# First additions of the norms' sums on VectorE, and the memory input loaded in four pieces

## The chip, the core and the metric

The kernel runs on one core of a Trainium2 chip. The core has five engines that run their own instruction lists side by side: TensorE for matmuls (PE in the rows, with its weight loads as PEld), VectorE (DVE), ScalarE (ACT), GpSimd (POOL) and SyncE (SP), which here only starts transfers. The engines wait for each other on semaphores, and each takes its instructions in order, so one that waits holds up all behind it. The metric is the time of one execution on the device in microseconds (us), as a median over runs.

## What is computed

Three blocks in float32, with 256 tokens of width 1024. Cut to what the change touches (the bodies of the attentions and of the state space model are left out):

```
def first_block(x, mem, ...):
    h = rmsnorm(x, mix_norm_g)
    y_s5 = s5(h @ w_in[u]); y_m = mlstm(h @ w_in[q, k, v, o, i, f])
    merged = sigmoid(gate) * (y_s5 @ w_br_s5) + sigmoid(gate) * (y_m @ w_br_m)
    x = x + merged @ w_out
    h = rmsnorm(x, x_norm_g)
    x = x + cross_attn(h, rmsnorm(mem, mem_norm_g), x_wq, x_wkv, x_wo)
    x = x + conv_ffn(rmsnorm(x, f_norm_g), ...)
    return rmsnorm(x, final_norm_g)
def even_block(x):  # differential and dilated attention, layer norm, conv FFN, layer norm
def odd_block(x):   # sparse and latent attention, layer norm, conv FFN, layer norm
```

`rmsnorm` divides by the root of the mean square over the 1024 features; `layer_norm` also takes the mean away.

## The kernel before

Activations lie feature-major: 8 tiles of 128 features by 256 tokens, so that x is `[128, 8, 256]`. A matmul in float32 is done as three matmuls in a rounded format: each operand is split in a high and a low part, and high x high, high x low and low x high are added up. For weights `wload` (L313) does it: SyncE fetches 128 x 1024 of a weight (512 KB) into `raw`, ScalarE copies it to `hi` (L321), VectorE makes `lo = raw - hi` (L322). `raw` has four buffers, `hi` and `lo` three each, so a weight is copied when the matmuls of the third before it are done. TensorE uses the parts at L329 to L331 (L338 to L340 for the token-major form), 24 matmuls for each pair.

A norm's sums over the 1024 features cross the partitions, and TensorE does that by a matmul with a column of ones (L469, tile `m`). Ahead of it `squares` has ScalarE square the tiles (L502, L506), two at a time for three pairs and two single ones, and `folded` (L484) adds them up: the first two pairs on GpSimd (L488), the third on VectorE (L490), the two halves (L492), a single one (L494). It is called 13 times: five root mean square norms, and four layer norms with two sums each. After L469 the reciprocal root is formed, and TensorE broadcasts it as a row over the partitions (L513), which becomes `rs` or `lnrow`.

The first block's mixer has, in this order on TensorE, the q and k groups (their results in `msg`, evicted by VectorE at L1706 and convolved into `mcv`), the groups that give v and the input and forget gates (`w_vif`, evicted to `vm` and `ifs`), and the rest of v and the output gate (`w_tm`, the first weight being hi_1026). Between them stand the small matmuls of the S5 state (L796 to L822), fed by VectorE (`so`, `hs`, L771, L772) and copied out by ScalarE (`CR`, `CN`, `KS`, `gs`, `gm`).

At its end `w_out` is applied in four column groups. Beside them `cross` (L981) begins: one transfer brings `mem`, 1 MB, on SyncE (L983). `rms_defer` (L581) then makes the split operand of the memory: `oh = mem * gain` on ScalarE (L583) and `ol` on VectorE (L584) for each of 8 tiles, and the squares, whose sums TensorE takes at L469 after the fourth column group. The projections use `oh`, `ol` right away, and the row is multiplied in afterwards. `mem` is a tile of a pool whose memory the mixer had, so its transfer waits until the mixer's last reader is done.

Who does what, and on which engine, is written in the program; the order of each engine's instructions is not. A planner (`schedule_with_timeline_sim=True`, L1861) walks the whole program with its own costs for every instruction and transfer and puts each engine's list in the order in which its model has them ready, with a higher priority for the weights (`WPRI`) and the layer norms (`LPRI`). A change in one line can so move instructions in other places.

Of the kernel before, what the change touches and what calls it, by code (L numbers as in the profile page):

```python
# [257 lines left out]
def _program(ctx, tc, nc, a, offs, dump):  # L258
    V, ACT, G, PE = nc.vector, nc.scalar, nc.gpsimd, nc.tensor
# [16 lines left out]
    def T(pl, shape, tag, dt=F32, **k):  # L276
        cnt[0] += 1
        return pl.tile(list(shape), dt, tag=tag, name="%s_%d" % (tag, cnt[0]), **k)

    mult, add, sub = ALU.mult, ALU.add, ALU.subtract  # L280
    stt = V.scalar_tensor_tensor
    tt = V.tensor_tensor
# [159 lines left out]
    def gemm_tm(name, ch, xh, xl, evac, cw=256):  # L442
        for j, c in enumerate(ch):
            if cw == 256:
                ps = T(pg, [P, 2, 256], "g")
                pt = [ps[:, t, :] for t in range(2)]
            else:
                pt = [T(pg, [P, cw], "g") for t in range(2)]
            step = 4 if cw == 256 else 3
            for k0 in range(0, 8, step):  # L450
                k1 = min(8, k0 + step)
                w = wload(name, c, cw * k0, cw * k1)
                for t in range(2):
                    tm_mm(pt[t], w, range(k0, k1), cw, t, xh, xl,
                          start=k0 == 0 and (t == 0 or cw > 256), stop=k1 == 8, skip=cw == 256)
            evac(j, ps if cw == 256 else pt)
# [27 lines left out]
    def folded(pairs, singles):  # L484
        if not pairs:
            return list(singles)
        acc = T(tp, [P, 2, S], "sqa", bufs=2)
        G.tensor_tensor(acc, pairs[0], pairs[1], op=add)  # L488
        for p in pairs[2:]:
            tt(acc, acc, p, op=add)  # L490
        one = acc[:, 0, :]
        tt(one, one, acc[:, 1, :], op=add)  # L492
        for p in singles[:-1]:
            tt(one, one, p, op=add)  # L494
        return [one, singles[-1]]
# [27 lines left out]
    def rms_cols(x, kt, eps, at=None):  # L523
        st = T(*(at or (pm,)), [P, 2], "g" if at else "m")
        col_sums(st, [folded(*squares(x, kt))])
        return rstd_cols(st, 2, kt * P, eps, "rms")

    def split(src, h, l, scale=None):
        if scale is None:
            ACT.copy(h, src)  # L530
            tt(l, src, h, op=sub)  # L531
        else:
            act(h, src, AF.Copy, scale=scale)
            stt(l, src, scale, h, op0=mult, op1=sub)
# [46 lines left out]
    def rms_defer(x, kt, g, eps, h, l, at=None):  # L581
        for k in range(kt):
            act(h[:, k, :], x[:, k, :], AF.Copy, scale=g[:, k:k + 1])  # L583
            stt(l[:, k, :], x[:, k, :], g[:, k:k + 1], h[:, k, :], op0=mult, op1=sub)  # L584
        r = rms_cols(x, kt, eps, at)
        rb = row_bcast([r[:, 0:1], r[:, 1:2]], at)
        rs = T(tp, [P, S], "rs")
        ACT.copy(rs, rb)
        return rs, r
# [13 lines left out]
    def bc2(rs):  # L603
        return bc(rs[:, None, :], [P, 2, S])

    def act_split():
        return T(hp, [P, 8, S], "xh", F32R), T(hp, [P, 8, S], "xl", F32R)
# [36 lines left out]
    def residual(x, xn):  # L644
        def ev(j, ps):
            tt(xn[:, 2 * j:2 * j + 2, :], ps, x[:, 2 * j:2 * j + 2, :], op=add)

        def single(n, ps):
            with tc.high_priority(LPRI):
                tt(xn[:, n, :], ps, x[:, n, :], op=add)  # L650

        def joint(n, ps):
            tt(xn[:, n, :], ps[:, 0, :], x[:, n, :], op=add)
            tt(xn[:, n, :], ps[:, 1, :], xn[:, n, :], op=add)
        return dict(evac=ev, single=single, joint=joint)
# [319 lines left out]
    def transpose_out(src_blocks, pl=None, tag="a"):  # L975
        tr = T(pl or pa, [P, 4, P], tag)
        for k, b in enumerate(src_blocks):
            PE.transpose(tr[:, k, :], b, ident)
        return tr

    def cross(ap_, x1):  # L981
        mem = T(ap_, [P, 8, S], "mem")
        nc.sync.dma_start(mem, a["mem"])  # L983
        memh, meml = T(ap_, [P, 8, S], "oh", F32R), T(ap_, [P, 8, S], "ol", F32R)
        ms_, mc_ = rms_defer(mem, 8, C["mem_norm_g"], 1e-6, memh, meml)
        kh, kl = [T(ap_, [P, 8, S], "k" + s, F32R) for s in "hl"]
        vh, vl = [T(ap_, [P, 2, D], "v" + s, F32R) for s in "hl"]

        def scaled(ps, rs, h, l):
            t = T(tp, [P, 2, S], "sq", bufs=3)  # L990
            tt(t, ps, bc2(rs), op=mult)
            split(t, h, l)

        def ev_k(j, ps):
            s2 = slice(2 * j, 2 * j + 2)
            scaled(ps, ms_, kh[:, s2, :], kl[:, s2, :])

        def ev_v(j, ps):
            for t in range(2):
                c = slice(j * 256, (j + 1) * 256)  # L1000
                split(ps[:, t, :], vh[:, t, c], vl[:, t, c], mc_[:, t:t + 1])

        gemm_pairs("x_wk", range(4), 8, memh, meml, ev_k)
        gemm_tm("x_wv", range(4), memh, meml, ev_v)
        xh, xl = act_split()
        rs, _ = rms_defer(x1, 8, C["x_norm_g"], 1e-6, xh, xl)
        qh, ql = [T(ap_, [P, 8, S], "q" + s, F32R) for s in "hl"]
        oh, ol = T(ap_, [P, 8, S], "oh", F32R), T(ap_, [P, 8, S], "ol", F32R)

        def x_scores(h, ps):  # L1010
            s2 = slice(2 * h, 2 * h + 2)
            scaled(ps, rs, qh[:, s2, :], ql[:, s2, :])
            sp = T(pa, [P, 2, S], "a")
            for t in range(2):
                for k in range(2 * h, 2 * h + 2):
                    tok = slice(t * P, (t + 1) * P)
                    mm(sp[:, t, :], qh[:, k, tok], kh[:, k, :], start=k % 2 == 0, stop=False)
                    mm(sp[:, t, :], qh[:, k, tok], kl[:, k, :], start=False, stop=False)
                    mm(sp[:, t, :], ql[:, k, tok], kh[:, k, :], start=False, stop=k % 2 == 1)
            nm = T(sm, [P, 2], "xnm")  # L1020
            V.reduce_max(nm, sp, axis=AX.X, negate=True)
            ts(nm, nm, 1.0 / 16, None, op0=mult)
            p = T(ap_, [P, 2, S], "xp", bufs=2)
            den = T(sm, [P, 2], "xden")
            for t in range(2):
                act(p[:, t, :], sp[:, t, :], AF.Exp, bias=nm[:, t:t + 1], scale=1.0 / 16, accum_out=den[:, t:t + 1])
            V.reciprocal(den, den)
            for t in range(2):
                ts(p[:, t, :], p[:, t, :], den[:, t:t + 1], None, op0=mult)
            return p  # L1030

        def x_out(h, p):
            tr = transpose_out([p[:, t, m * P:(m + 1) * P] for m in range(2) for t in range(2)])
            pT = T(ap_, [P, 2, 2, S], "xpT", F32R, bufs=2)
            split(tr.rearrange("p (m t) b -> p m (t b)", m=2), pT[:, 0], pT[:, 1])
            o = T(pm, [P, 2, S], "m")
            for d in range(2):
                for m in range(2):
                    c = slice(h * 256 + d * P, h * 256 + (d + 1) * P)
                    mm(o[:, d, :], vh[:, m, c], pT[:, 0, m, :], start=m == 0, stop=False)  # L1040
                    mm(o[:, d, :], vh[:, m, c], pT[:, 1, m, :], start=False, stop=False)
                    mm(o[:, d, :], vl[:, m, c], pT[:, 0, m, :], start=False, stop=m == 1)
            split(o, oh[:, 2 * h:2 * h + 2, :], ol[:, 2 * h:2 * h + 2, :])

        held = []

        def ev(h, ps):
            held.append((h, x_scores(h, ps)))
            if h >= 1:
                x_out(*held.pop(0))  # L1050

        gemm_pairs("x_wq", range(4), 8, xh, xl, ev)
        x_out(*held.pop(0))
        x2 = T(xp, [P, 8, S], "x")
        gemm_pairs("x_wo", range(4), 8, oh, ol, **residual(x1, x2))
        return x2

    def ln_stats(z):
        with tc.high_priority(LPRI):
            st = T(pm, [P, 4], "m")  # L1060
            col_sums(st, [folded(*tiles(z, 8)), folded(*squares(z, 8))])
        return st
# [726 lines left out]
    with ExitStack() as ph:  # L1789
        x2 = cross(pool(ph, "cx", 1), x1)  # L1790
# [75 lines left out]
```

## Time and profile before

| | us |
|---|---|
| runs shown, median of 3 | 1204.42 (1202.92 to 1205.2) |
| profiled execution | 1202.35 |
| its span, first to last instruction | 1200.6 |
| mean granted TensorE clock (1 is full) | 0.992 |

| engine | busy us | share | instructions |
|---|---|---|---|
| TensorE | 1160.7 | 97% | 8794 |
| VectorE | 911.7 | 76% | 1757 |
| ScalarE | 712.8 | 59% | 1301 |
| GpSimd | 73.4 | 6% | 80 |

The busy share is an average over stages. Where a stage has TensorE busy throughout, no other engine can be what bounds it; where TensorE has a hole, the row gives the instruction that it waited for. Times in the rows count from the start of the span.

### The profile page before, as it was taken

The numbers are of one execution on the slowest core, as the hardware profiler recorded it, in microseconds if no ns is written. First come the engines' busy times: TensorE is split into PE (matmuls) and PEld (weight loads), VectorE is DVE, ScalarE is ACT, GpSimd is POOL, SyncE is SP. The second block draws the span as 40 slices with busy tenths as digits, with TensorE's granted clock in tenths as the row PEclk, the third lists the DMA queues.
The fourth block names the chain that finished last, engine by engine and source line by source line (L and its number), as shares of the span: only waits on it lengthen the run. The fifth ranks groups of instructions, "written<-read, shape, count | busy, mean of one in ns | idle before, by whom it ended". The sixth has DMA issues, their size and how long they took to land.

```text
span 1200.6 us, 22550 instructions
## 1 busy us (share of the span) xinstructions
PE 1160.7 (97%) x8794; PEld 1076.0 (90%) x8794; DVE 911.7 (76%) x1757; ACT 712.8 (59%) x1301; POOL 73.4 (6%) x80
## 2 busy tenths in 40 slices
PE   7999999999999999999999899999999999999997
PEld 6889989999999999899988888888988789888886
DVE  8979856866689887666564898876697768988754
ACT  5684644655566765446355686654685666776541
POOL 4400000100000000000001000001000001000010
PEclk9999999999999999999999999999999999999999
DMA  7524535654356555656522546666863125665561
GB/s 260 166 71 143 166 116 179 221 181 157 103 177 195 182 181 175 191 167 232 170 92 93 191 161 193 187 175 197 284 215 118 57 70 190 191 203 188 168 199 35
DMA packets 61273, 199.35 MB, mean 166 GB/s; under 512 B 8502, under 2 KB 12398, under 8 KB 60910
## 3 DMA queue, kind: packets, MB, share of 16 engines
q1 hardware_dynamic: 54864, 191.60, 49.8%
q10 hardware_dynamic: 6302, 6.32, 1.7%
q8 instruction: 69, 1.13, 0.4%
q14 instruction: 38, 0.31, 0.1%
HBM read 196.28 MB, written 1.60 MB: 165 GB/s over the span
## 4 chain that ended last, share of the span: by engine, by line
PE 87%; DVE 6%; ACT 4%; issue 2%; DMA 1%; POOL 0%; SPq 0%; DVEq 0%; ACTq 0%
PE a L408 11%; PE g L330 10%; PE g L329 10%; PE g L331 10%; PE g L408 8%; PE a L410 6%; PE g L410 4%; PE a L329 3%; PE a L330 3%; PE a L331 3%; PE g L340 2%; PE g L338 2%; PE g L339 2%; DVE lo L322 2%; PE m L1167 1%
## 5 line engine op out<-in xcount | busy, mean ns | idle before, releaser
L321 ACT CAST hi<-raw 128x1024 fp32r<-128x1024 f32 (+3 forms) x359 | 363.9, 1020 | 312.9 <-PE g L330 102.1
L322 DVE TENSOR_TENSOR lo<-raw,hi 128x1024 fp32r<-128x1024 f32 (+3 forms) x359 | 427.5, 1196 | 153.4 <-ACT hi L321 147.8
L329 PE MATMUL g<-xh,hi 128*128 128x256 f32 (+1 forms) x616 | 177.0, 288 | 8.7 <-ACT xh L583 8.4
L330 PE MATMUL g<-xl,hi 128*128 128x256 f32 (+1 forms) x624 | 179.5, 288 | 0.2
L331 PE MATMUL g<-xh,lo 128*128 128x256 f32 (+1 forms) x616 | 175.8, 286 | 1.2 <-DVE lo L322 1.2
L329 PEld LDWEIGHTS g<-xh,hi 128*128 128x128 f32 x616 | 118.2, 192 | 10.2 <-ACT xh L583 8.7
L330 PEld LDWEIGHTS g<-xl,hi 128*128 128x128 f32 x624 | 120.1, 192 | 1.4 <-DVE xl L584 0.7
L408 PE MATMUL a<-nhl,hi 128*128 128x512 f32 x336 | 119.0, 398 | 1.2 <-DVE sq L1110 1.2
L331 PEld LDWEIGHTS g<-xh,lo 128*128 128x128 f32 x616 | 117.7, 191 | 2.0 <-DVE lo L322 1.6
L410 PE MATMUL a<-nhl,lo 128*128 128x256 f32 x336 | 93.9, 279 | 0.0
L408 PE MATMUL a<-mx,hi 128*128 128x512 f32 x264 | 92.5, 396 | 0.0
L408 PE MATMUL g<-nhl,hi 128*128 128x512 f32 x240 | 83.8, 394 | 0.0
L408 PEld LDWEIGHTS a<-nhl,hi 128*128 128x128 f32 x336 | 63.6, 189 | 15.9 <-issue 1.4
L410 PE MATMUL a<-mx,lo 128*128 128x256 f32 x264 | 73.2, 279 | 0.0
L408 PE MATMUL g<-mx,hi 128*128 128x512 f32 x198 | 69.7, 397 | 0.0
L410 PE MATMUL g<-nhl,lo 128*128 128x256 f32 x240 | 66.5, 278 | 0.7 <-DVE lo L322 0.7
L410 PEld LDWEIGHTS a<-nhl,lo 128*128 128x128 f32 x336 | 63.7, 190 | 0.1
L408 PEld LDWEIGHTS a<-mx,hi 128*128 128x128 f32 x264 | 49.3, 188 | 11.5
L410 PE MATMUL g<-mx,lo 128*128 128x256 f32 x198 | 55.4, 280 | 0.0
L408 PEld LDWEIGHTS g<-nhl,hi 128*128 128x128 f32 x240 | 44.9, 188 | 10.2
L329 PE MATMUL a<-nhl,hi 128*128 128x256 f32 x176 | 50.2, 285 | 3.4 <-ACT sqa L1092 2.8
L330 PE MATMUL a<-nhl,hi 128*128 128x256 f32 x176 | 50.0, 284 | 1.0 <-DVE nhl L531 1.0
(637 smaller groups left out, 3088.3 us busy)
## 6 DMA issues: line engine op xcount, KB each, us to landing
raw<-g_up SPq DMA_DIRECT2D x88, 512.0 KB, 3.8
raw<-f_up SPq DMA_DIRECT2D x44, 512.0 KB, 3.4
raw<-g_dn SPq DMA_DIRECT2D x32, 512.0 KB, 3.6
raw<-w_fm SPq DMA_DIRECT2D x27, 512.0 KB, 3.6
raw<-ev_fm SPq DMA_DIRECT2D x20, 512.0 KB, 4.0
raw<-f_dn SPq DMA_DIRECT2D x16, 512.0 KB, 3.7
raw<-od_fm SPq DMA_DIRECT2D x14, 512.0 KB, 3.6
raw<-g_dn SPq DMA_DIRECT2D x16, 384.0 KB, 3.3
```

The costliest lines, as they stand in the source:

```text
L321: ACT.copy(hi, raw)
L322: tt(lo, raw, hi, op=sub)
L329: mm(ps, hi[:, o:o + P], xh[:, k, :], start=start and k == 0, stop=False, skip_group_check=skip)
L330: mm(ps, hi[:, o:o + P], xl[:, k, :], start=False, stop=False, skip_group_check=skip)
L331: mm(ps, lo[:, o:o + P], xh[:, k, :], start=False, stop=stop and k == kt - 1, skip_group_check=skip)
L338: mm(ps, xh[:, k, t], hi[:, wsl], start=start and j == 0, stop=False, skip_group_check=skip)
L339: mm(ps, xh[:, k, t], lo[:, wsl], start=False, stop=False, skip_group_check=skip)
L340: mm(ps, xl[:, k, t], hi[:, wsl], start=False, stop=stop and j == len(ks) - 1, skip_group_check=skip)
L408: mm(f2, hi[:, o], X[:, k].rearrange("p a s -> p (a s)"), start=first and j == 0, stop=False, skip_group_check=True)
L410: mm(ps[:, 0, :], lo[:, o], X[:, k, 0, :], start=False, stop=last and j == len(ks) - 1, skip_group_check=True)
L1167: mm(o[64 * r:64 * r + 64, :], v0, pT[:, 0:S], start=first, stop=False, skip_group_check=True)
```

## The change

The first addition of each of the 13 sums is issued on VectorE instead of GpSimd, with the same operands. The memory input is fetched by four transfers of two tiles each, 256 KB, where there was one of 1 MB. The tile `mem` is the same, and each reader waits for the piece that it reads.

```
--- before.py
+++ after.py
@@ -485,7 +485,7 @@
         if not pairs:
             return list(singles)
         acc = T(tp, [P, 2, S], "sqa", bufs=2)
-        G.tensor_tensor(acc, pairs[0], pairs[1], op=add)
+        tt(acc, pairs[0], pairs[1], op=add)
         for p in pairs[2:]:
             tt(acc, acc, p, op=add)
         one = acc[:, 0, :]
@@ -980,7 +980,8 @@
 
     def cross(ap_, x1):
         mem = T(ap_, [P, 8, S], "mem")
-        nc.sync.dma_start(mem, a["mem"])
+        for k in range(0, 8, 2):
+            nc.sync.dma_start(mem[:, k:k + 2, :], a["mem"][:, k:k + 2, :])
         memh, meml = T(ap_, [P, 8, S], "oh", F32R), T(ap_, [P, 8, S], "ol", F32R)
         ms_, mc_ = rms_defer(mem, 8, C["mem_norm_g"], 1e-6, memh, meml)
         kh, kl = [T(ap_, [P, 8, S], "k" + s, F32R) for s in "hl"]
```

From the changed line on, line numbers above 983 are one higher, and the numbers of tiles from 2785 on are three higher (oh_2784 is oh_2787).

The planner's lists change with it, in three places that matter below. Before, on VectorE in the mixer, at the instructions ahead of msg_568, the eviction of the second q and k group:

```order
L771 TENSOR_TENSOR hs_681<-cz_374,cs_20_137 128x512
L1717 SCALAR_TENSOR_TENSOR x_431<-msg_504,mcv_495 128x512
L771 TENSOR_TENSOR so_814<-pz_350,cs_20_137 128x640
L322 TENSOR_TENSOR lo_957<-raw_954,hi_956 128x528
L772 TENSOR_TENSOR so_680<-so_680,hs_681 128x512
L1706 TENSOR_TENSOR msg_568<-g_507,rs_184 128x512
```

and the same place now:

```order
L1718 SCALAR_TENSOR_TENSOR x_431<-msg_504,mcv_495 128x512
L771 TENSOR_TENSOR so_680<-cz_374,cs_20_137 128x512
L322 TENSOR_TENSOR lo_933<-raw_930,hi_932 128x792
L772 TENSOR_TENSOR so_671<-so_671,hs_672 128x512
L1707 TENSOR_TENSOR msg_568<-g_507,rs_184 128x512
L322 TENSOR_TENSOR lo_957<-raw_954,hi_956 128x528
L771 TENSOR_TENSOR hs_681<-cz_374,cs_20_137 128x512
L771 TENSOR_TENSOR so_814<-pz_350,cs_20_137 128x640
L772 TENSOR_TENSOR so_680<-so_680,hs_681 128x512
```

Four instructions (hs_681, so_814, lo_957 and the addition into so_680) that stood ahead of msg_568 now stand behind it. On TensorE the four matmuls at L796 that stood ahead of the group that needs msg_568's bank now stand inside that group; on ScalarE hi_1026 stood behind the second half's weights for the S5 state and now stands ahead of them, behind the copies to CR, KS and CN.

Before, on ScalarE at the end of the mixer, where xh is the last split of the merged branches, hi_2616, hi_2648, hi_2678 and hi_2709 are weights of `w_out`, and oh is the memory's operand:

```order
L533 ACTIVATE xh_2378<-gs_1487 128x512 x2
L321 CAST hi_2616<-raw_2614 128x1024
L321 CAST hi_2648<-raw_2646 128x1024
L321 CAST hi_2678<-raw_2676 128x1024
L583 ACTIVATE oh_2784<-mem_2782,consts_91 128x256 x8
L502 ACTIVATE sq_2803<-mem_2782 128x512
L502 ACTIVATE sq_2805<-mem_2782 128x512
L502 ACTIVATE sq_2807<-mem_2782 128x512
L506 ACTIVATE sq_441_2809<-mem_2782 128x256
L506 ACTIVATE sq_442_2811<-mem_2782 128x256
L321 CAST hi_2709<-raw_2707 128x1024
```

and now:

```order
L533 ACTIVATE xh_2378<-gs_1487 128x512 x2
L583 ACTIVATE oh_2787<-mem_2782,consts_91 128x256 x2
L502 ACTIVATE sq_2806<-mem_2782 128x512
L321 CAST hi_2616<-raw_2614 128x1024
L583 ACTIVATE oh_2787<-mem_2782,consts_91 128x256 x2
L502 ACTIVATE sq_2808<-mem_2782 128x512
L583 ACTIVATE oh_2787<-mem_2782,consts_91 128x256 x2
L502 ACTIVATE sq_2810<-mem_2782 128x512
L583 ACTIVATE oh_2787<-mem_2782,consts_91 128x256 x2
L506 ACTIVATE sq_441_2812<-mem_2782 128x256
L506 ACTIVATE sq_442_2814<-mem_2782 128x256
L321 CAST hi_2648<-raw_2646 128x1024
```

Three weight copies stood ahead of everything that reads the memory; now the first of them stands behind the first piece's three readers, and the other two behind all readers. After hi_2648 follow hi_2678 and hi_2709.

Before, on TensorE in the same stage, where g_2583, g_2645 and g_2713 are the second and third column group of `w_out` and the first half of the fourth:

```order
L331 MATMUL g_2583<-xh_2378,lo_2617 128x256
L329 MATMUL g_2645<-xh_2378,hi_2648 128x256
L330 MATMUL g_2645<-xl_2379,hi_2648 128x256
L331 MATMUL g_2645<-xh_2378,lo_2649 128x256
L329 MATMUL g_2645<-xh_2378,hi_2648 128x256
```

and now:

```order
L331 MATMUL g_2583<-xh_2378,lo_2617 128x256
L329 MATMUL g_2645<-xh_2378,hi_2648 128x256
L330 MATMUL g_2645<-xl_2379,hi_2648 128x256
L329 MATMUL g_2713<-xh_2378,hi_2709 128x256
L330 MATMUL g_2713<-xl_2379,hi_2709 128x256
L331 MATMUL g_2645<-xh_2378,lo_2649 128x256
L329 MATMUL g_2645<-xh_2378,hi_2648 128x256
```

Two matmuls that need hi_2709 were moved from behind the third column group to its third place. In the two layer norms ahead of the second block's FFNs (at 650 and 990 us) the matmuls at L513 stand 12 and 13 matmuls later than before among the same ones.

## Rows read from the trace of the kernel before

**Rows 1.** Page, parts 1 and 4: busy time of each engine; the chain that ended last.

```profile
PE 1160.7 (97%) x8794; PEld 1076.0 (90%) x8794; DVE 911.7 (76%) x1757; ACT 712.8 (59%) x1301; POOL 73.4 (6%) x80
...
PE 87%; DVE 6%; ACT 4%; issue 2%; DMA 1%; POOL 0%; SPq 0%; DVEq 0%; ACTq 0%
```

**Rows 2.** Line L488 alone: its first form (min/median/max ns), and who waited.

```profile
L488 POOL TENSOR_TENSOR sqa<-sq,sq x9: 1277/1475/2340, 9.9 to 1160.3; 128x512 f32<-128x512 f32 x9
...
  DVE sqa L490: 1.2, 1
```

**Rows 3.** Timeline around 653 us: GpSimd (start us, us, instruction).

```profile
653.36 1.47 POOL L488 TENSOR_TENSOR sqa<-x 128x512 f32<-128x512 f32 x1 [32.95 <-DVE x L1147]
```

**Rows 4.** Timeline: VectorE beside it, and the first row's form at 994 us.

```profile
653.20 1.92 DVE L548 SCALAR_TENSOR_TENSOR xl<-x,consts,xh 128x256 fp32r<-128x256 f32 x2
...
658.81 0.68 DVE L490 TENSOR_TENSOR sqa<-sqa,x 128x512 f32<-128x512 f32 x1
...
994.61 0.87 DVE L548 SCALAR_TENSOR_TENSOR xl<-x,consts,xh 128x256 fp32r<-128x256 f32 x2
```

**Rows 5.** Timeline in the mixer: TensorE, its waits in brackets with their releaser.

```profile
48.83 0.27 PE L796 MATMUL a<-consts,w 128*128 128x128 f32 x1
...
52.43 0.56 PE L338 MATMUL g<-hi,xh 128*128 128x264 f32 x1 [3.00 <-DVE msg L1706]
...
63.62 0.33 PE L796 MATMUL a<-consts,w 128*128 128x128 f32 x1 [1.21 <-ACT w L789]
...
67.42 0.33 PE L796 MATMUL a<-consts,w 128*128 128x128 f32 x1
...
72.46 0.39 PE L339 MATMUL g<-lo,xh 128*128 128x256 f32 x1 [1.12 <-DVE lo L322]
```

**Rows 6.** Timeline in the mixer: VectorE ahead of the second of these rows.

```profile
49.65 0.81 DVE L771 TENSOR_TENSOR so<-pz,cs 128x640 f32<-128x640 f32 x1
50.39 0.69 DVE L322 TENSOR_TENSOR lo<-raw,hi 128x528 fp32r<-128x528 f32 x1
51.01 0.68 DVE L772 TENSOR_TENSOR so<-so,hs 128x512 f32<-128x512 f32 x1
```

**Rows 7.** Stretches: us; PE busy, PEld, DVE, ACT, POOL; granted clock, DMA share, GB/s.

```profile
52.40:55.60 3.20, 3.17 (x14) 3.20 (x15) 3.17 (x5) 3.13 (x7) 0.00 (x0) 0.50 0.56 209
...
205.00:222.00 17.00, 16.55 (x138) 16.34 (x137) 14.36 (x22) 11.79 (x20) 2.04 (x1) 1.00 0.60 197
...
919.20:922.60 3.40, 3.40 (x18) 3.40 (x17) 0.70 (x3) 0.37 (x1) 0.00 (x0) 0.50 0.50 159
```

**Rows 8.** Timeline of TensorE ahead of the last of these stretches.

```profile
918.89 0.38 PE L513 MATMUL g<-consts,rmsr 128*128 128x128 f32 x1 [1.33 <-POOL rmsr L520]
```

**Rows 9.** Timeline of SyncE: the issue of the memory input.

```profile
202.40 0.33 SPq L983 DMA_DIRECT2D mem<-mem  x1
```

**Rows 10.** Transfers: count, KB each, median us from issue to landing.

```profile
mem<-mem SPq DMA_DIRECT2D x1, 1024.0 KB, 4.8
...
out<-x SPq DMA_DIRECT2D x3, 256.0 KB, 2.1
...
raw<-w_vif SPq DMA_DIRECT2D x1, 264.0 KB, 2.7
```

**Rows 11.** Timeline of ScalarE around the memory input.

```profile
203.31 1.05 ACT L321 CAST hi<-raw 128x1024 fp32r<-128x1024 f32 x1 [1.73 <-PE g L330]
...
208.12 3.30 ACT L583 ACTIVATE oh<-mem,consts 128x256 fp32r<-128x256 f32 x8
...
211.33 1.66 ACT L502 ACTIVATE sq<-mem 128x512 f32<-128x512 f32 x3
...
212.90 0.71 ACT L506 ACTIVATE sq<-mem 128x256 f32<-128x256 f32 x2
```

**Rows 12.** Timeline of VectorE: the low part after the first of these rows.

```profile
204.39 1.22 DVE L322 TENSOR_TENSOR lo<-raw,hi 128x1024 fp32r<-128x1024 f32 x1 [2.08 <-ACT hi L321]
```

**Rows 13.** Timeline of TensorE: the sums of the memory's norm.

```profile
222.02 0.17 PE L469 MATMUL m<-ones,sqa 128*128 128x1 f32 x1
```

More of the change, by code (lines that the diff above doesn't have):

```diff
@@ L487, in folded @@
         acc = T(tp, [P, 2, S], "sqa", bufs=2)
-        G.tensor_tensor(acc, pairs[0], pairs[1], op=add)
+        tt(acc, pairs[0], pairs[1], op=add)
         for p in pairs[2:]:
@@ L982, in cross @@
         mem = T(ap_, [P, 8, S], "mem")
-        nc.sync.dma_start(mem, a["mem"])
+        for k in range(0, 8, 2):
+            nc.sync.dma_start(mem[:, k:k + 2, :], a["mem"][:, k:k + 2, :])
         memh, meml = T(ap_, [P, 8, S], "oh", F32R), T(ap_, [P, 8, S], "ol", F32R)
```

## Prediction, made before the changed kernel was run

> **What bounds the kernel now.** I read the page's busy times and its chain first, then the waits of TensorE, and then the timeline of each stretch in which the change moves something. TensorE is busy 97% of the span and holds 87% of the chain that ended last; VectorE is busy 76% and holds 6% of that chain [rows 1]. The reader is to see that the kernel is a queue of matmuls with a few holes. An edit that saves or costs VectorE time counts only where TensorE then waits longer or shorter, so every term below is a hole of TensorE: the sum of what opens, less what closes.
>
> **Part one, the additions on VectorE.** Thirteen adds leave GpSimd. There one took 1475 ns in the middle case, and VectorE waited for one of them once, 1.2 us [rows 2]. On VectorE the next add of the same shape stands with 0.68 us, of which some 0.6 us is its step to the following instruction [rows 4]; 13 x 0.6 = 7.8 us more work for an engine that is idle 24% of the span. TensorE covers it, except where the adds alter the order; without that cover it would be 7.8 us at most.
>
> Beside a GpSimd add VectorE itself runs longer: while the add of 1.47 us stood at 653.36 us [rows 3], two instructions that elsewhere took 0.87 us took 1.92 us, 1.05 us more [rows 4]. So the move also gives VectorE something back. Priced by that row it is 13 x (1.05 - 0.6) = 5.9 us, which I keep as the gain's bound. I take 0 for the forecast, because TensorE waited for VectorE in none of the rows around those adds and the chain gives VectorE 6%. The Trainium skill (SBUF — State Buffer, "SBUF: two separate sides") goes further: GpSimd and a VectorE instruction with two inputs in SBUF share one pair of ports, and whichever starts first holds it for its whole instruction. The stretch at 653 us agrees in kind, with 1.05 us of a 1.47 us add. By that rule all of each add would come back to VectorE; what that makes of the time is the second rival below.
>
> The wait of 1.2 us that goes [rows 2] was VectorE's at 214 us; TensorE's only hole in that stage is 17.00 - 16.55 = 0.45 us [rows 7], so I count nothing for it.
>
> **The mixer, 48 to 80 us: 0.5 us won.** TensorE had waited 3.00 us for msg, then 1.21 us and 1.12 us [rows 5]. After the first of these the granted clock was 0.50 for 3.2 us, which is the lower of its two levels, 1.2 GHz [rows 7]; half of 3.2 us, 1.6 us, is lost by it. Together 3.00 + 1.21 + 1.12 + 1.6 = 6.9 us. In the new order msg stands ahead of four instructions that ran before it: 0.74 (so at 49.65), 0.62 (lo) and 0.60 (so at 51.01), each the step to the next start [rows 6], and hs, of the last one's width, at 0.60. Msg comes 2.56 us sooner. The group that needs it would start at 52.43 - 2.56 = 49.87 us, and TensorE reaches it at 48.83 us, since the four matmuls at L796 now stand behind it: a wait of 1.0 us.
>
> The lead is then spent. The second V, input and forget group no longer waits for the next msg, and TensorE runs through it; after it stands the group of hi_1026. ScalarE now has that copy behind ten or so copies of the second half of the S5 state; counting them through, hi_1026 comes at 63.1 us if none waits and at 64.9 us if each waits for its matmul, and its lo 1.2 us later [rows 12]. TensorE is through with everything ahead at about 61.5 us: 49.87 plus the 15.0 us that the same work took (52.43 to 67.4 us), less its wait of 1.21 and the 1.6 of the clock, less 0.5 for four matmuls at L796 that now come later [rows 5]. The new hole is 2.8 to 4.6 us. If the clock falls after it as it did after 3.00 us, 1.7 us come on top. New holes 1.0 + 2.8 = 3.8 to 1.0 + 4.6 + 1.7 = 7.3 us, against 6.9 us: from 3.1 us won to 0.4 us lost. I take 0.5 us won, near the losing end, since each of the copies waits for a matmul that just moved.
>
> **Part two, the memory input in four pieces: 4.2 us lost, and 1.7 us for the clock.** The transfer could not leave before 202.40 us [rows 9], for it takes over memory that the split of the merge branches still reads, and that is unchanged. Whole, it landed after 4.8 us; a store of 256 KB took 2.1 us and a weight load of 264 KB 2.7 us [rows 10]. For the first piece I take 2.7, the nearest in kind and size: it lands at 205.1 us. Bounds 204.5 and 207.2 us.
>
> In front of that landing ScalarE used to do hi_2616 (203.31 us) and two more weights, and all eight oh (3.30 us, 0.41 each) came after [rows 11]. Now hi_2616 stands behind two oh and one square. ScalarE waits in order, so hi_2616 starts at 205.1 + 0.82 + 0.55 (a third of 1.66) = 206.5 us, ends at 207.5, and its lo, 1.22 us [rows 12], at 208.7. Between 205 and 222 us TensorE ran 138 matmuls in 16.55 us, 0.12 us each [rows 7]. Counted back from the norm's sums at 222.02 us [rows 13], with the 120 matmuls between (14.3 us) and the hole of 0.45, it needs that lo at 207.3 us. First hole: 1.4 us. It then has 22 matmuls, to 211.3 us. ScalarE meanwhile does six oh (2.46), two squares (1.1) and the two narrow ones (0.71) [rows 11], 4.3 us, and then hi_2648: ready at 212.8 us. Second hole: 1.5 us. Next stand two matmuls of the fourth column group, which need hi_2709, two more copies of 1.0 us: 214.8 us after two matmuls at 213.05. Third hole: 1.75 us. From there 92 matmuls run without a wait. 1.4 + 1.5 + 1.75 - 0.45 = 4.2 us lost. With the first landing at 204.5 us it is 3.6; if the piece lands with the whole, at 207.2, it is 6.3 us. The weights' issue on SyncE behind the pieces is later by three more issues of 0.33 us [rows 9]; the next one was at 205.65 us by then, so nothing is behind it.
>
> TensorE's clock was 1.00 here [rows 7]. It fell to 0.50 for 3.4 us after a wait of 1.33 us that a shorter one preceded [rows 7, 8]. Two holes of 1.5 and 1.75 us with 0.24 us of work between them are more than that, so I take a fall: half of 3.4, 1.7 us; at its lower bound nothing.
>
> **The layer norms of the second block: 1.3 us lost.** In the norms at 650 and 990 us the four VectorE adds change the order that TensorE has: the norm's row matmuls stand 12 and 13 matmuls later among the same work. At 0.12 us that is 1.5 us later for the row that the norm's output is made from. In the first, ScalarE and VectorE have an extra weight copy to put in that time, and I take 0.5 us of it; in the second nothing of the kind is put there, so I take 0.8. Bounds 0 and 1.5 us for each. All other norms keep TensorE's order or have cover.
>
> **The sum.** -0.5 + 4.2 + 1.7 + 0.5 + 0.8 = +6.7 us. The profiled execution took 1202.35 us, 1.75 us around its span of 1200.6; the median of the runs shown, 1204.42 us, is 2.07 us above it. 1202.35 + 6.7 = 1209.05, and 1211.1 us on the scale of the median.
>
> **The rivals.** (1) Every open value falls to the kind side: the mixer wins 3.1 us, the first piece lands at 204.5 us, the clock holds, and the norms hide their shift: -3.1 + 3.6 = +0.5 us, 1204.9 us. For it: the ranges are real, and the clock did not fall after 1.21 us at 63.62. Against: it wants four things together. 0.16.
>
> (2) Faster: VectorE was blocked by GpSimd's adds, and the adds' time comes back where TensorE waits for weights' low parts. 13 x 1.475 = 19.2 us come back [rows 2] and 7.8 go, 11.4 us net; if all reach TensorE, 6.7 - 11.4 = -4.7 us: 1199.7 us. For it: the stretch of 1.05 us [rows 4]. Against: TensorE's holes are elsewhere [rows 5, 7], and VectorE has 6% of the chain. It decides once more than 6.7 us of the 11.4 reach TensorE, over half. 0.10. The rule of the Trainium skill named above would have it so.
>
> (3) The split does not do what it says: the pieces share the queue and the first lands no sooner than the whole did. The memory stage then loses 6.3 + 1.7 us: +8.8 us, 1213.2 us. For it: nothing leaves before 202.40 us, and other weights are in flight (DMA share 0.60 [rows 7]). Against: the 2.1 and 2.7 us of small transfers [rows 10]. 0.14.
>
> **How the numbers follow.** The forecast, with its own neighbourhood from 1207 to 1213 us, has 0.60. A change of 0.2%, 2.4 us, is about what a measurement can tell from none. Slower holds the forecast and (3), 0.74; within it (1), 0.16; faster (2), 0.10. The range from 1203.5 to 1215 us leaves out (2) and the far end of (3).
>
> **What the profile will show.** Right: ScalarE idle from about 202.5 to 205 us with hi_2616 after the first square, three holes of TensorE at 207, 211 and 213 us, and the sums of the memory's norm some 4 us later than the mixer's shift alone makes them; a hole at 61 to 66 us. Wrong: hi_2616 at 203 us; a first piece landed before 204 us; TensorE without a hole in either stretch, or VectorE's lo steps clearly denser over the whole span, which would be rival (2).

## The result, and the profile after

The change made the kernel slower: 1213.26 us, median of 4 runs (1211.49 to 1215.43), against 1204.81 us for the kernel before on the same chip; the ratio is 1.0075 with a 95% interval from 1.0053 to 1.0098. The profiled execution took 1215.43 us with a span of 1213.6 us and a mean granted clock of 0.987. The page, busy time of each engine and then the chain that ended last, answers to [rows 1]:

```profile
PE 1168.5 (96%) x8794; PEld 1080.9 (89%) x8794; DVE 909.2 (75%) x1770; ACT 712.4 (59%) x1301; POOL 50.9 (4%) x67
...
PE 88%; DVE 5%; ACT 4%; issue 2%; DMA 2%; SPq 0%; POOL 0%; DVEq 0%; ACTq 0%
```

VectorE has 13 instructions more and is busy 2.5 us less. The line L488 alone (count, min/median/max ns) shows what an addition costs on VectorE, against the 1475 ns of [rows 2]:

```profile
L488 DVE TENSOR_TENSOR sqa<-sq,sq x9: 677/684/693, 9.4 to 1173.5; 128x512 f32<-128x512 f32 x9
L488 DVE TENSOR_TENSOR sqa<-x x4: 684/684/687, 661.4 to 1172.9; 128x512 f32<-128x512 f32 x4
```

On GpSimd the four additions of the second form, which [rows 2] leaves out, took longer than the nine of the first:

```profile
L488 POOL TENSOR_TENSOR sqa<-x x4: 1469/1876/2323, 653.4 to 1158.1; 128x512 f32<-128x512 f32 x4
```

All thirteen took 22.8 us there. On VectorE 13 x 0.684 = 8.9 us came in and the total fell by 2.5, so VectorE's other work became 11.4 us shorter: that much the second rival's source gave back, net 2.5 us. The order of VectorE's list moves its busy time as well (913.7 us in e2 below, with every addition still on GpSimd), so these figures are good to some 2 us. TensorE's share of the chain grew, and the reader turns to its holes. In the mixer (start, duration, instruction, the wait before it in brackets), against [rows 5]:

```profile
48.47 0.36 PE L338 MATMUL g<-hi,xh 128*128 128x264 f32 x1 [1.56 <-DVE msg L1707]
63.52 0.58 PE L338 MATMUL g<-hi,xh 128*128 128x256 f32 x1 [3.12 <-ACT hi L321]
65.04 0.58 PE L339 MATMUL g<-lo,xh 128*128 128x256 f32 x1 [0.94 <-DVE lo L322]
...
153.97 0.53 PE L969 MATMUL a<-consts,hn 128*128 128x128 f32 x2 [0.76 <-DVE hn L968]
155.50 0.33 PE L969 MATMUL a<-consts,hn 128*128 128x128 f32 x1 [0.50 <-DVE hn L968]
```

The wait for msg shrank, a wait for hi_1026 opened, and at 154 us stand two waits, 1.26 us together, that the kernel before does not have. At the memory input SyncE issues four pieces; ScalarE then waits for the first, and TensorE waits three times. SyncE, ScalarE, TensorE, and the transfers (KB each, median us to landing):

```profile
202.80 2.79 SPq L984 DMA_DIRECT2D mem<-mem  x4
...
205.91 0.91 ACT L583 ACTIVATE oh<-mem,consts 128x256 fp32r<-128x256 f32 x2 [3.92 <-DMA mem<-mem]
206.73 0.61 ACT L502 ACTIVATE sq<-mem 128x512 f32<-128x512 f32 x1
207.25 1.03 ACT L321 CAST hi<-raw 128x1024 fp32r<-128x1024 f32 x1
...
212.34 2.93 ACT L321 CAST hi<-raw 128x1024 fp32r<-128x1024 f32 x3
```

```profile
208.33 0.39 PE L329 MATMUL g<-xh,hi 128*128 128x256 f32 x1 [1.07 <-ACT hi L321]
209.59 0.58 PE L331 MATMUL g<-xh,lo 128*128 128x256 f32 x1 [0.76 <-DVE lo L322]
...
213.74 0.28 PE L329 MATMUL g<-xh,hi 128*128 128x256 f32 x1
...
215.32 0.39 PE L329 MATMUL g<-xh,hi 128*128 128x256 f32 x1 [1.18 <-ACT hi L321]
...
mem<-mem SPq DMA_DIRECT2D x4, 256.0 KB, 4.4
```

The copy at 207.25 is hi_2616, which stood at 203.31 [rows 11]; the three from 212.34 are hi_2648, hi_2678 and hi_2709. The first two waits are for hi_2616 and its low part. The matmul at 213.74, the 23rd from 209.59 on, is the first that needs hi_2648, and it does not wait. The third wait ends at 215.32, when the last of the three copies is done (212.34 + 2.93 = 215.27): it is for hi_2709. The stretches, columns as in [rows 7], show the clock:

```profile
62.70:69.30 6.60, 4.84 (x21) 4.55 (x22) 5.96 (x11) 6.48 (x13) 0.66 (x1) 0.50 0.43 145
205.00:222.00 17.00, 13.98 (x99) 13.17 (x98) 12.72 (x20) 10.98 (x19) 0.00 (x0) 0.90 0.54 173
208.90:212.30 3.40, 2.71 (x12) 2.71 (x13) 3.40 (x8) 3.40 (x9) 0.00 (x0) 0.58 0.47 152
622.30:625.70 3.40, 3.40 (x19) 3.40 (x18) 2.25 (x7) 2.15 (x5) 0.26 (x1) 0.52 0.16 62
```

From 205 to 222 us TensorE got through 99 matmuls where it had done 138, at a clock of 0.90 instead of 1.00. The fall at 622 us has no wait before it. Last, the layer norms of the second block; TensorE in the kernel before, and then after:

```profile
684.61 0.36 PE L329 MATMUL a<-nhl,hi 128*128 128x256 f32 x1 [2.76 <-ACT sqa L1092]
...
1020.22 0.36 PE L329 MATMUL a<-nhl,hi 128*128 128x256 f32 x1 [0.46 <-DVE wgb L1107]
```

```profile
692.87 0.36 PE L329 MATMUL a<-nhl,hi 128*128 128x256 f32 x1 [3.66 <-ACT hi L321]
...
1031.76 0.36 PE L329 MATMUL a<-nhl,hi 128*128 128x256 f32 x1 [0.96 <-ACT sqa L1093]
1033.07 0.47 PE L408 MATMUL a<-nhl,hi 128*128 128x512 f32 x1 [0.36 <-DVE sq L1111]
1034.53 0.47 PE L408 MATMUL a<-nhl,hi 128*128 128x512 f32 x1 [0.41 <-DVE sq L1111]
```

A table by stage makes the traces comparable. The bounds are TensorE instructions that every trace has with a like wait: the first matmul, L331 at the end of the mixer (199.77 us before), L329 ahead of the f_norm stage (314.90), L1167 (645.68), L329 of the first layer norm (684.61), L978 (976.15) and L330 of the second (1023.62). Microseconds; runs of the experiments below stand in it too. Each stage has the same matmuls in every kernel, with one exception: where the layer norms' additions are on VectorE, four matmuls stand ahead of the end of the last stage that stood behind it. TensorE in that stage, before and after, with the columns of [rows 7]:

```profile
976.15:1023.61 47.46, 45.83 (x372) 43.84 (x372) 37.66 (x66) 30.59 (x52) 5.97 (x6) 1.00 0.49 163
```

```profile
987.15:1036.50 49.35, 46.57 (x376) 44.47 (x376) 37.47 (x70) 31.03 (x53) 3.35 (x4) 1.00 0.49 164
```

TensorE is idle there for 1.63 us before and 2.78 after, 1.15 us more; the other 0.7 us of the column's 1.9 are the four matmuls, moved and not lost.

| kernel | mixer | memory | f_norm, FFN | norm 650 | 684 to 976 | norm 990 |
|---|---|---|---|---|---|---|
| before | 191.33 | 115.13 | 330.78 | 38.93 | 291.54 | 47.47 |
| changed | 192.24 | 119.81 | 333.13 | 39.75 | 294.29 | 49.35 |
| changed, second trace | 191.54 | 119.79 | 331.37 | 39.84 | 295.57 | 49.38 |
| e1: additions alone | 190.50 | 122.37 | 331.44 | 39.89 | 294.11 | 49.35 |
| e2: pieces alone | 191.03 | 116.25 | 330.78 | 38.93 | 294.21 | 47.46 |
| e4: layer norms back | 190.23 | 120.95 | 331.37 | 38.90 | 294.14 | 47.48 |
| e5: weights first | 190.99 | 116.25 | 334.64 | 39.78 | 294.09 | 49.37 |
| n1: first norm alone | 190.58 | 122.10 | 332.56 | 38.93 | 294.05 | 47.46 |
| n2: all but the first | 189.20 | 118.24 | 331.37 | 39.84 | 295.88 | 49.35 |
| n3: six, same order | 188.64 | 115.34 | 330.78 | 38.92 | 294.63 | 47.47 |
| n4: pieces, all but the first | 191.23 | 117.65 | 331.37 | 39.75 | 296.19 | 49.35 |
| n5: memory's norm alone | 188.73 | 116.32 | 333.83 | 38.93 | 294.91 | 47.47 |
| n6: layer norms alone | 188.66 | 115.16 | 330.78 | 39.80 | 293.92 | 49.35 |

### The profile page after: what moved, and what is told of

It reads as the page before. It is cut to its first block, busy times and chain, and to the rows that moved or that the text cites. A ratio compares the mean times of both kernels' runs of the same rounds, so it can differ in the third digit from the quotient of the medians.

```text
span 1213.6 us, 22533 instructions
## 1 busy us (share of the span) xinstructions
PE 1168.5 (96%) x8794; PEld 1080.9 (89%) x8794; DVE 909.2 (75%) x1770; ACT 712.4 (59%) x1301; POOL 50.9 (4%) x67
## 4 chain that ended last, share of the span: by engine, by line
PE 88%; DVE 5%; ACT 4%; issue 2%; DMA 2%; SPq 0%; POOL 0%; DVEq 0%; ACTq 0%
PE a L408 11%; PE g L330 11%; PE g L329 11%; PE g L331 11%; PE g L408 8%; PE a L410 6%; PE g L410 4%; PE a L330 3%; PE a L329 3%; PE a L331 3%; PE g L338 2%; PE g L340 2%; PE g L339 2%; DVE lo L322 1%; PE m L1168 1%
## 5 line engine op out<-in xcount | busy, mean ns | idle before, releaser
L322 DVE TENSOR_TENSOR lo<-raw,hi 128x1024 fp32r<-128x1024 f32 (+3 forms) x359 | 424.1, 1187 | 166.4 <-ACT hi L321 161.8
L329 PE MATMUL g<-xh,hi 128*128 128x256 f32 (+1 forms) x616 | 176.4, 287 | 10.8 <-ACT xh L583 7.9
L330 PE MATMUL g<-xl,hi 128*128 128x256 f32 (+1 forms) x624 | 179.1, 287 | 0.1
L331 PE MATMUL g<-xh,lo 128*128 128x256 f32 (+1 forms) x616 | 175.5, 286 | 1.5 <-DVE lo L322 1.5
L329 PEld LDWEIGHTS g<-xh,hi 128*128 128x128 f32 x616 | 117.7, 191 | 13.0 <-ACT xh L583 8.2
L408 PE MATMUL a<-nhl,hi 128*128 128x512 f32 x336 | 121.7, 404 | 2.1 <-DVE xl L531 1.3
L330 PEld LDWEIGHTS g<-xl,hi 128*128 128x128 f32 x624 | 119.3, 191 | 1.3 <-DVE xl L584 0.5
L331 PEld LDWEIGHTS g<-xh,lo 128*128 128x128 f32 x616 | 117.1, 191 | 2.5 <-DVE lo L322 2.1
L329 PE MATMUL a<-nhl,hi 128*128 128x256 f32 x176 | 49.9, 286 | 4.6 <-ACT hi L321 3.7
L330 PE MATMUL a<-nhl,hi 128*128 128x256 f32 x176 | 49.8, 285 | 1.0 <-DVE nhl L531 1.0
```

Source lines behind the costliest of these rows:

```text
L322: tt(lo, raw, hi, op=sub)
L329: mm(ps, hi[:, o:o + P], xh[:, k, :], start=start and k == 0, stop=False, skip_group_check=skip)
L330: mm(ps, hi[:, o:o + P], xl[:, k, :], start=False, stop=False, skip_group_check=skip)
L331: mm(ps, lo[:, o:o + P], xh[:, k, :], start=False, stop=stop and k == kt - 1, skip_group_check=skip)
L408: mm(f2, hi[:, o], X[:, k].rearrange("p a s -> p (a s)"), start=first and j == 0, stop=False, skip_group_check=True)
```

## The experiments

The rival to settle first: is the loss made by the pieces, as the prediction's second part has it, or by the additions? In the expectations hi_417, hi_421, hi_424 and hi_427 are hi_2616, hi_2648, hi_2678 and hi_2709.

**e1, the additions alone:** line L488 as changed, the memory loaded whole.

```
-        G.tensor_tensor(acc, pairs[0], pairs[1], op=add)
+        tt(acc, pairs[0], pairs[1], op=add)
```

> Only the additions are moved to VectorE; the memory input stays one transfer. Theory (what counts is where each engine's list puts its instructions): mixer +0.4 us and the two layer norms of the second block +5.5 us, as in the traces of the changed kernel; and in the memory stage this kernel's ScalarE list has all eight oh and the squares ahead of hi_421, so hi_421 waits for the whole 1 MB: landing 202.4 + 4.8 = 207.2 us, then 5.7 us of work, ready at 213.9 us against 209.9 us needed, and its lo after it: 5.0 us of holes less 0.45, and 1.7 us for the clock, +6.2 us. Sum about +12 us: 1213 to 1218 us. Rival A (the split is what costs, the additions only move work beside TensorE): 1204 to 1207 us. Rival B (VectorE freed from GpSimd's adds makes it faster): below 1202 us.

**e2, the pieces alone:** L488 as before, the loop over four pieces at L983.

```
-        nc.sync.dma_start(mem, a["mem"])
+        for k in range(0, 8, 2):
+            nc.sync.dma_start(mem[:, k:k + 2, :], a["mem"][:, k:k + 2, :])
```

> Only the transfer is split; the additions stay on GpSimd. Theory: mixer and layer norms as before; in the memory stage this list has hi_417 ahead of all readers of the memory and hi_421 behind five oh and two squares of the first three pieces: ready at 209.7 us against 209.9 us needed, so only its lo may be late, 0.8 us at most. 1204 to 1206.5 us, no change from before. Rival A (the split costs the 4 to 6 us of the memory stage by itself): 1209 to 1212 us.

Measured: e1 1213.6 us, ratio 1.0081 [1.0067, 1.0095]; e2 1205.4 us, 1.0014 [1.0001, 1.0027]; the kernel before in that job had 1202.99 us. Both are inside the ranges expected, e1 at the low end and not by the terms of its sum: the memory stage lost 7.2 us (6.2 expected) and the two layer norms 2.8 (5.5). The additions alone cost as much as the whole change, and the pieces alone little. The two do not add up: the memory stage loses 7.2 us with the additions alone and 4.7 with the pieces as well, so the pieces give 2.5 us back. ScalarE in e2 shows why they cost little without the additions:

```profile
202.55 1.05 ACT L321 CAST hi<-raw 128x1024 fp32r<-128x1024 f32 x1 [1.73 <-PE g L330]
204.61 0.91 ACT L583 ACTIVATE oh<-mem,consts 128x256 fp32r<-128x256 f32 x2 [1.01 <-DMA mem<-mem]
...
208.37 1.03 ACT L321 CAST hi<-raw 128x1024 fp32r<-128x1024 f32 x1
...
210.24 1.03 ACT L321 CAST hi<-raw 128x1024 fp32r<-128x1024 f32 x1
```

hi_2616 stands ahead of the first piece, and hi_2648 and hi_2678 between the pieces' readers, at 208.37 and 210.24 us.

**e5, the weights first:** the changed kernel, with the memory's gain and the scale of its squares taken from a VectorE instruction that reads the mixer's output x1, so that ScalarE has hi_2616, hi_2648 and hi_2678 ahead of every reader of the memory.

```
-        ms_, mc_ = rms_defer(mem, 8, C["mem_norm_g"], 1e-6, memh, meml)
+        gl, on = T(ap_, [P, 8], "gl"), T(ap_, [P, 1], "on")
+        stt(gl, x1[:, 0, 0:8], 0.0, C["mem_norm_g"], op0=mult, op1=add)
+        ts(on, x1[:, 0, 0:1], 0.0, 1.0, op0=mult, op1=add)
+        ms_, mc_ = rms_defer(mem, 8, gl, 1e-6, memh, meml, scale=on)
```

> The changed kernel, in which the memory's gain and a one (for the squares) are first passed through an instruction that reads the first eviction of the output projection, so that ScalarE's list again has hi_417, hi_421 and hi_424 ahead of all readers of the memory; four pieces and VectorE's additions stay. Theory: the three holes of the memory stage and the clock's fall after them go, 4.7 us in the traces; the mixer's and the norms' part stays: 1207.5 to 1210.5 us. Rival (the pieces themselves cost, by their landing or their issue, and not the order on ScalarE): 1212 to 1215 us.

Measured: 1208.18 us, 1.0049 [1.0032, 1.0065]. The memory stage fell to 116.25 us, with 13 additions and four pieces in place. So the order of ScalarE's copies makes 3.6 us of that stage's 4.7; 1.1 us stay, as in e2.

**e4, the layer norms back on GpSimd:** the changed kernel with the eight additions of the layer norms as before.

```
-        tt(acc, pairs[0], pairs[1], op=add)
+        (G.tensor_tensor if ln else tt)(acc, pairs[0], pairs[1], op=add)
```

> The changed kernel with the eight additions of the layer norms back on GpSimd. Theory: the layer norms cost 5.5 us of the change in the traces, and they go: 1207 to 1210.5 us, with TensorE's lists at 650 and 990 us as before. Rival (the clock's falls and the memory stage are all of the loss, the norms' shift is hidden): 1212 to 1215 us, as the changed kernel.

Measured: 1212.05 us, 1.0075 [1.0053, 1.0096], a miss that lies in the rival's range. The ratio is that of the changed kernel, so the time shows nothing won, with an interval of some 2.6 us to either side. In the trace the stages of both norms are back at 38.90 and 47.48 us, but the memory stage took 120.95 us, 1.1 us more than in the changed kernel. The 5.5 us expected for the norms were too many.

Which of the thirteen additions moves what, then? The next four, and two more, choose additions by their number in the program (0 the first norm, 1 the memory's, 2 to 4 the other root mean square norms, 5 to 12 the layer norms):

```
-    def folded(pairs, singles):
+    def folded(pairs, singles, nth=itertools.count()):
...
-        G.tensor_tensor(acc, pairs[0], pairs[1], op=add)
+        (tt if next(nth) in (0,) else G.tensor_tensor)(acc, pairs[0], pairs[1], op=add)
```

**n1** has (0,); **n2** has 1 to 12; **n3** has (2, 4, 7, 8, 11, 12); **n4** is the changed kernel with 1 to 12.

> Of the thirteen additions only the first norm's, at 10 us, is on VectorE; the memory input is loaded whole. Theory A (this one addition, through the planner's order, makes the memory stage's loss: on ScalarE hi_421 and hi_424 stand behind everything that reads the memory): the stage from 199 to 321 us takes 121 to 123 us against 115.1 of before, ScalarE holds TensorE for 3 to 4.5 us near 212 us, the clock falls there, and the whole is +6 to +8 us, 1209 to 1212.5 us. Rival B (the loss is made by the additions near where it shows, or by VectorE's extra work): the stage takes 115 to 117 us, 1203 to 1206 us.

> Twelve additions on VectorE, the first norm's on GpSimd; the memory input is loaded whole. Theory A: ScalarE has hi_417, hi_421 and hi_424 ahead of the memory's readers as before, the memory stage takes 115 to 117 us; what is left of the loss is the f_norm stage (+0.6) and the layer norms (+0.9 and +1.9 at 690 and 1030 us): +2.5 to +4.5 us, 1205.5 to 1208.5 us. Rival B: 121 us or more for the memory stage and 1211 to 1215 us.

> Six additions on VectorE (those of the norms x1 and x3, and the second of each layer norm's pair for two norms and both for a third), chosen since TensorE's and ScalarE's orders are then those of the kernel before, row for row; the memory input is loaded whole. Theory A (only the order costs, and VectorE's time is off the path): no change, 1202 to 1206 us, with VectorE's busy time some 5 us less than before's. Rival C (the time that GpSimd's additions take from VectorE comes back to TensorE): six times 1.475 less six times 0.6 us, 5.3 us: 1198 to 1200.5 us.

> The changed kernel with the first norm's addition alone put back on GpSimd. Theory A: hi_421 and hi_424 then stand among the memory's readers on ScalarE, the memory stage takes 115.5 to 117.5 us against 119.8 of the changed kernel, and the whole is 1206 to 1209.5 us. Rival B: the stage stays at 119 us or more and the whole at 1211 to 1215 us.

Measured, against 1203.33 us: n1 1213.2 us, 1.0085 [1.0069, 1.0101]; n2 1210.98, 1.0063 [1.0043, 1.0082]; n3 1202.54, 0.9994 [0.9983, 1.0004]; n4 1208.17, 1.0042 [1.0027, 1.0057].

n1 is the surprise of the study: a single addition at 10 us, of 0.68 us, costs as much as all thirteen. The memory stage is inside the expected range, the time 0.7 us above it. ScalarE, TensorE and the stretch behind in n1:

```profile
202.26 1.05 ACT L321 CAST hi<-raw 128x1024 fp32r<-128x1024 f32 x1 [1.77 <-PE g L330]
206.26 3.31 ACT L583 ACTIVATE oh<-mem,consts 128x256 fp32r<-128x256 f32 x8 [2.95 <-DMA mem<-mem]
209.47 1.65 ACT L502 ACTIVATE sq<-mem 128x512 f32<-128x512 f32 x3
211.03 0.70 ACT L506 ACTIVATE sq<-mem 128x256 f32<-128x256 f32 x2
211.65 2.92 ACT L321 CAST hi<-raw 128x1024 fp32r<-128x1024 f32 x3
```

```profile
212.72 0.58 PE L329 MATMUL g<-xh,hi 128*128 128x256 f32 x1 [4.13 <-ACT hi L321]
...
213.00:219.40 6.40, 5.94 (x29) 5.64 (x30) 3.87 (x5) 2.10 (x3) 0.00 (x0) 0.55 0.61 190
```

The chain reads upward: TensorE waited 4.13 us for hi_2648; ScalarE had it behind the thirteen instructions that read the memory (3.31 + 1.65 + 0.70 us) and 2.95 us of waiting for the transfer, where the list of the kernel before has hi_2648 and hi_2678 ahead of all that. Behind the hole the clock was at 0.55 for 6.4 us, which costs 2.9 us more. In all, 7.0 us of that stage.

n2 lacks that order, as expected, and yet its time and its memory stage came out above their ranges. What was not expected is TensorE's wait for the memory's norm, first below, and GpSimd's reciprocal root that released it. Then the root, and VectorE beside it, in n2 and in the changed kernel:

```profile
231.75 0.71 PE L513 MATMUL m<-consts,rmsr 128*128 128x128 f32 x4 [3.22 <-POOL rmsr L520]
...
226.28 5.42 POOL L520 TENSOR_TENSOR rmsr<-rmsms,mhalf 128x2 f32<-128x2 f32 x1 [79.94 <-ACT rmsms L518]
...
226.52 4.62 DVE L322 TENSOR_TENSOR lo<-raw,hi 128x1024 fp32r<-128x1024 f32 x4
```

```profile
232.60 1.04 POOL L520 TENSOR_TENSOR rmsr<-rmsms,mhalf 128x2 f32<-128x2 f32 x1 [80.90 <-ACT rmsms L518]
...
231.42 3.25 DVE L584 SCALAR_TENSOR_TENSOR xl<-x,consts,xh 128x256 fp32r<-128x256 f32 x8
```

The same instruction took 5.42 us in n2 and 1.04 us in the changed kernel, after 80 us of idleness in both. What differs is VectorE's list: in n2 four low parts of weights run there one behind the other, and the root ends at 231.70 us, 0.56 us after the last of them. So n2's 3.1 us are a matter of order too, on VectorE this time.

n3 answers the second rival in part. TensorE and ScalarE have the order of before, six additions left GpSimd, and nothing happened to the time: had the rival's 5.3 us come back and reached TensorE, the ratio would have been 0.996. But VectorE's busy time did not drop by the 5 us that the expectation names. The page of n3 has it at exactly the figure of [rows 1]:

```profile
PE 1162.3 (97%) x8794; PEld 1076.5 (90%) x8794; DVE 911.7 (76%) x1763; ACT 712.8 (59%) x1301; POOL 61.3 (5%) x74
```

Six additions of 0.69 us went in, so some 4 us came back, as much as was added. VectorE had no net time to hand on, and whether TensorE would have got it is not tested by n3. The kernel before bounds it, by TensorE's waits for the weights' low parts (us in total, times, longest):

```profile
PE g L331 <- DVE lo L322: 1.2, 2, 0.8
...
PE g L339 <- DVE lo L322: 1.1, 1, 1.1
...
PE g L410 <- DVE lo L322: 0.7, 1, 0.7
```

That is 3.0 us in the whole kernel, all that the rival could have won on its path. n4 points the same way as n1: with the first addition back on GpSimd the changed kernel's memory stage falls from 119.8 to 117.65 us and its ratio from 1.0075 to 1.0042. The time is inside its range, the stage 0.15 us above. TensorE still waits there for one weight and its low part, 1.93 and 0.76 us, so the pieces and the twelve other additions keep 2.5 us of that stage's loss.

The last three: **n5** has (1,) and **n6** has 5 to 12, both with the memory whole; **n7** is the changed kernel once more.

> Of the thirteen additions only that of the memory's norm is on VectorE; the memory is loaded whole. Theory A (each addition costs by what it moves in the order): ScalarE has one more weight copy ahead of the step from the norm's sums to its mean, so that TensorE waits about 3 us for the norm's factor near 232 us as with the twelve additions (3.22 us there), the memory stage takes 118 to 119 us against 115.1, and the whole is +2.5 to +5.5 us: 1206 to 1209 us. Rival B (one addition more or less is nothing, the hole at 232 us came from the others): 115 to 116 us for the stage, 1202.5 to 1205 us.

> Only the eight additions of the layer norms on VectorE, the other five on GpSimd; the memory is loaded whole. Theory A (the two layer norms cost what their holes show, 0.9 and 1.9 us, and half a fall of the clock where one is made longer): +2 to +4.5 us, 1205 to 1207.8 us. Rival D (as when these eight were put back in the changed kernel, their part is hardly more than 1 us): up to +1.5 us, 1202.5 to 1204.9 us.

> The changed kernel once more, for a second trace. If the clock's falls without a wait ahead of them (at 622 us in the first trace) are a matter of chance, they come at other places or not at all, and the span moves by 1.7 us for each, 1208 to 1214 us; if they belong to the change, 622 us shows one again. The waits in the mixer, the memory stage and the norms stand as in the first trace, within 0.3 us each.

Measured, against 1203.13 us: n5 1205.78 us, 1.0026 [1.0009, 1.0043]; n6 1207.49, 1.0041 [1.0026, 1.0056]; n7 1214.19 us, one run, span 1212.4. In n5 the root on GpSimd took 4.28 us, TensorE waited 1.34 us for it, and the stage lost 1.2 us: neither theory's 3 nor nothing, and the time lies between the two ranges. My reason for that wait was wrong: what is late is GpSimd's instruction, again beside low parts on VectorE, not a weight copy ahead of it on ScalarE. n6 is a hit by its time. Its trace shows 0.87 and 1.88 us in the two norms, 0.7 of the second being the moved matmuls. The 2.0 us that are left are less than the 4.4 us of the medians; the rest is not explained.

n7 settled the fall at 622 us. Its stretches at 622, and at 912 us, where the first trace of the same kernel has a clock of 1.00:

```profile
622.30:625.70 3.40, 3.40 (x32) 3.40 (x31) 1.98 (x6) 2.13 (x6) 1.64 (x1) 1.00 0.01 2
...
912.60:916.00 3.40, 3.40 (x18) 3.40 (x18) 3.33 (x22) 3.04 (x14) 0.00 (x0) 0.53 0.42 121
```

The same kernel has the fall at one place in one execution and at another in the next. At 622 us neither trace has a wait of TensorE in the 30 us before. At 912 us both have two just before, 0.53 and 0.2 us, and only the second trace has the fall. The waits in the mixer, the memory stage and the norms stood as in the first trace, within 0.3 us.

## Why the prediction was right, and where it was not

The time, 1211.1 us, was 2.2 us short, and the direction was right. It is that near by some luck: the memory stage was taken 1.2 us too large, and the other terms together 3.1 us too small. Term by term:

- **Memory stage, +4.2 and +1.7 for the clock.** Measured: +4.7 in both traces of the changed kernel. The first piece landed at 205.9 us (205.1 had been taken), and the first hole was 1.07 + 0.76 = 1.8 us (1.4 taken). The clock fell, but behind this first hole, not behind the third. TensorE, slowed, then reached hi_2648 only when it was there: the second hole (1.5 taken) did not open. The third, for hi_2709, did, at 1.18 us (1.75 taken). The mechanism held, with a size 1.2 us too large.
- **Its heading failed.** The prediction booked this loss under the memory input in four pieces. By e1, e2 and n1 it belongs for the most part to the first norm's addition, 195 us earlier, which alone costs 7.0 us there; with it, the pieces make the loss smaller, and without it, in n4, 2.5 us stay. The list of the changed kernel shows what stands late, and not which of two edits put it there. What was missing is the list of each edit by itself. Rival 3 is out, since the first piece landed 3.1 us after its issue; e1, where the memory does come whole, shows what it would have been: 7.2 us in that stage, against the 8.0 that it was given.
- **Mixer, -0.5.** This is the step that failed: its bounds went from 3.1 us won to 0.4 lost. The new hole of 2.8 to 4.6 us for hi_1026 and its low part came, at 3.12 + 0.94 = 4.1 us; the wait for msg left 1.56 us (1.0 taken). What it lacked is the 1.26 us at 154 us. In the six traces with the first addition on VectorE the mixer takes 191.0 us on average, in the seven others 189.8: about 1.2 us lost, some 0.4 of it by a lower clock. The trace of before, at 191.33, was a slow example of its own order (n3: 188.64): the clock stood at its lower level for 6.8 us of the mixer there, and for 3.4 us in n3.
- **Layer norms, +0.5 and +0.8.** The first measured +0.8 to +0.9. The second is +1.9 in the table, of which 1.15 us are waits: 0.96 us where there was 0.46, and 0.36 and 0.41 us anew for the groups behind the norm. Both are inside the bounds of 0 and 1.5 us, and were taken too small.
- **All other norms, 0.** They do not all keep TensorE's order: the f_norm stage loses 0.6 us (330.78 to 331.37) wherever the additions change it.

1.2 + 4.7 + 0.6 + 0.9 + 1.15 = 8.6 us; the ratio says 0.75% of 1203.3, 9.0 us [6.4, 11.8]. The pair of profiled spans differs by 13.0, some 4 us more. That excess is the fall at 622 us and the stretch from 684 to 976 us, which took 291.54 us in the trace of before and 293.9 to 296.2 in every other, n3 with the same order among them. The clock stood at its lower level for 6.8 us of that stretch in the trace of before and for 10.2 to 13.7 us in the twelve others, which makes 1.7 to 3.4 us of the difference.

- **Rival 2, VectorE freed.** The effect is real but smaller than this rival had it: 11.4 us came back, 0.88 us for each addition, and 8.9 went, so 2.5 net. The 19.2 us that it started from were too few, since they took the 1475 ns of one form for all thirteen; together they had 22.8. Nor was there a path for its 11.4 us: TensorE's waits for low parts were 3.0 us in all, and it needed more than 6.7. By the Trainium skill's rule of the ports that GpSimd and VectorE share (SBUF — State Buffer, "SBUF: two separate sides") all of each addition would have come back if VectorE always had an instruction with two inputs in SBUF to run; the trace agrees in kind, with half of it (11.4 of 22.8 us).

Summed like this, the stages of the other kernels come out within the intervals of their times or, for n1 (8.2 us of 10.2 [8.3, 12.2]), next to it. What stays open is n6, 2.0 us of 4.9 [3.1, 6.7], and that the effects of single edits don't add up: n1 and n2 together would be 1.5%, against e1's 0.81%. In the memory stage 2.9 us of that is n2's slow root, which e1 does not have (1.03 us); no run separates the rest. No version beat the kernel before.

## What to carry to other kernels

Where a planner orders the lists, an edit's first cost is the order. A single 0.7 us instruction moved at 10 us changed ScalarE's list at 205 us and cost 7 us there; so compare the lists of each edit alone, look for copies that TensorE needs and that now stand behind a wait for a transfer, and take a move that leaves TensorE's and ScalarE's lists the same as safe, as n3 was, but not as a gain. Time given back to an engine counts at most for as much as TensorE waits for that engine, and that sum stands in the profile of before: here 3.0 us for VectorE's low parts.

## What the runs showed of the hardware

- The granted clock's falls are partly chance. With identical instructions in the stretch, the clock fell at 622 us in one trace of the changed kernel (0.52 over 3.40 us) and was 1.00 there in the other. TensorE was busy throughout (3.40 of 3.40 us) and had not waited for 30 us. Such a fall costs about 1.7 us, half of 3.4: n1, with the matmuls of before in the same order and one fall in the f_norm stage, took 332.56 us there against 330.78. A pair of traces can so differ by several us for no reason in the code, and differences of that size are read from medians over many runs.
- One GpSimd instruction, the reciprocal root of 128 x 2 values, took 4.28 and 5.42 us in n5 and n2 and 0.76 to 1.36 us in the eleven other traces. Idleness does not explain it (80.9 us before a root of 1.04 us). The two long roots are the only ones with more than one low part on VectorE (L322, 1.22 us each) beside them: in n2 the root ended 0.56 us after the last of four without a pause, in n5 0.56 us after the third, behind which VectorE paused for 0.27 us. With one low part beside it, the first norm's root took 1.72 to 1.77 us in three traces (before, e1, n6) and ended 0.56 to 0.60 us after it; alone, roots took 0.70 us. So the root seems to wait until VectorE's low parts leave a pause. These are coincidences in thirteen traces; no run moved the low parts alone.
